# W1's first column pair of each MLP's first quarter as seven half products instead of eight, with the activation combinations formed during the output projection

## The chip, the cores and the metric

The kernel runs as one program on one core of a Trainium2 chip. The metric is the device time of one execution in microseconds (us), lower is better. TensorE (PE) does the matrix products, VectorE (DVE) and ScalarE (ACT) the elementwise work, GpSimd (POOL) a little of it, and the DMA queues of SyncE (SP) and POOL load the weights.

## The reference

A two layer decoder trunk on 256 tokens with 2048 columns in float32. Layer 0 mixes with gated linear attention, layer 1 with sliding window attention on a shared K/V, and each mixer is followed by a square-relu MLP with 8192 hidden columns. What matters here is the border between a mixer's output projection and the MLP behind it, which the program passes twice:

```
h = h + gla_mixer(u, ...)          # ends in  o @ w_o   (layer 1: swa_sink_mixer, o @ w_o)
h = h + sqrelu_mlp(rmsnorm(h, norm_mlp[layer]), mlp_w1[layer], mlp_w2[layer])

def sqrelu_mlp(h, w1, w2):
    u = jax.nn.relu(h @ w1)
    return (u * u) @ w2
```

## The kernel before

**Precision.** Each float32 weight tile is split by `halve` (L107) into a rounded part `wh` (an ACT cast, L116) and a rest `wl` (a DVE subtraction, L117). Activations are kept as such pairs too (`act`: `ah`, `al`). A product is the three matmuls ah wh, ah wl and al wh. In most products the activation is the stationary operand (128 tokens) and 512 columns of the weight move through.

**The MLP.** `mlp` (L952) works in four quarters of 2048 hidden columns. A quarter forms two pairs of 512 columns of W1 and then multiplies with that quarter's rows of W2 (`seven`, L1094). A column pair of W1 is a product of 256 tokens with 2048 x 1024 weights. In `two_columns` (L985, class `Seven`, L219) the upper half of it, a 2 x 2 block product (token halves by two blocks of 512 rows by two blocks of columns), takes seven half products in place of eight. A "product" is 12 matmuls (4 rows of 128, 3 matmuls each), a "plain" step 24, and a pair has seven products and four plain steps, 180 matmuls with 512 moving columns. The steps are named in an order string: "1 21 3 7 5 31 x 20 e 6 2 30 a 4" (a digit is a product, two digits are a plain step on rows block and column block, "x" adds weights for later products). Product 1 uses the weight tile `wx`, which its own queue loads in two halves of 512 KB (`load_x`, L241). Later products use combinations of the weights (accumulating DMAs on POOL, additions on DVE) and of the activations (`es`, tiles `cmb`). The pair's outputs have tokens on the partitions and are turned by 16 transposes (`turn`, L996).

The first pair of the first quarter of each MLP is the exception. There `gemm_wide` (L190) keeps the weight stationary and moves the activations: for each of two columns 64 steps of one matmul with 512 moving columns (ah and al side by side) and one with 256. Its outputs need no transposes, but the row scale of the norm must lie along the free axis, which `along` (L362) does with two matmuls. `pause` (L1058) adds two tiny ones. While it runs, `form_sums` (L972) forms the activation combinations for the other quarters into `cmb` tiles and stores them in DRAM (`kept`), and quarters 1 to 3 fetch them from there with two POOL DMAs each (`fetch_sums`, L979).

**The output projection.** `residual` (L881) multiplies with w_o. Its second column pair is a `Seven` too, in the order "1 21 31 3 7 e 5 20 30 6 2 4"; its last steps are product 6, product 2 and product 4. Product 6 ends the columns of block 3: DVE adds them to the residual (`p56`, L912: `vp`, two `xs`, and as the last one `xs` minus `vp`, L910), then `operands` (L848) turns and scales them into the MLP's `act`. Block 2 follows after product 4. So act 3 is ready before act 2.

**What sets the order.** The code is written step by step with `later` (work put off by so many half steps). A scheduler then places the instructions on each engine, and a wait for a semaphore stands on each instruction that needs one. Each engine and each queue runs its list in order. Tiles come from pools. A mixer’s pool (`g2`/`ga` in layer 0, `s2`/`sa` in layer 1) is closed behind the output projection, and the MLP's pool `mp` (`wx`, `wy`, `u`, `h`) is laid over its memory. The tiles `ws`, `wh`, `wl` and `act` come from pools that live through the whole program.

Of the kernel before, what the change touches and what calls it, by code (L numbers as in the profile page):

```python
# [16 lines left out]
P = 128  # L17
# [22 lines left out]
CS = 13  # L40
RS = 4
MX = 2
COMB = (1, 3)
ORDERS = "1 21 3 7 31 e 5 20 30 6 2 4", "21 1 31 3 7 e 5 20 30 6 2 4"
KEEP = 5, 7
OPS = 7, 9
# [5 lines left out]
def yoco_kernel(ctx: ExitStack, tc: tile.TileContext, x, norms, mlp_w1, mlp_w2, a_w_in, w_glr, w_gate, a_g_o, a_w_o,  # L52
# [12 lines left out]
    def bank(shape, tag, dtype=F32):  # L65
        return ps[tag].tile(shape, dtype, name=tag, tag=tag)
# [94 lines left out]
    def gemm_sta(src, act, evac, widths=(P, P, P, P), first=None):  # L161
# [4 lines left out]
        def run(kq):  # L166
# [16 lines left out]
            if kq == 3:  # L183
                for b, acc in enumerate(accs):
                    evac(b, acc)
        return run

    wide_tags = [("acc",) * 4, ("tp", "ms", "tp", "ms")]

    def gemm_wide(src, act, evac):  # L190

        accs = []
        tags = wide_tags[0]
        wide_tags.reverse()

        def run(kq):
            if kq == 0:
                accs.extend(bank([P, 2, T], tag) for tag in tags)
            halves = split_w(src(kq))
            ah, _, a = act[kq]  # L200
            order = [(k, f) for k in range(4) for f in range(4)]
            if kq == 0:
                order = [(k, 2 * h + f) for h in range(2) for k in range(4) for f in range(2)]
            for i, (k, f) in enumerate(order):
                wh, wl = (w[:, f * P:(f + 1) * P] for w in halves[k])
                mm(accs[f].rearrange("p u t -> p (u t)"), wh, a[:, k].rearrange("p u t -> p (u t)"),
                   kq == 0 and k == 0, False, skip_group_check=True)
                mm(accs[f][:, 1], wl, ah[:, k], False, kq == 3 and k == 3, skip_group_check=True)
                if i == 7:
                    tick()  # L210
            tick()
            if kq == 3:
                for f in range(4):
                    evac(f, accs[f])
        return run
# [146 lines left out]
    def along(rb, r):  # L362
# [6 lines left out]
        nc.scalar.copy(out=rb, in_=pt[:, :T])  # L369

    def twice(rb):
        return rb.rearrange("p (o n) -> p o n", o=1).broadcast_to([P, 2, T])


# [505 lines left out]

    def residual(w, act, gains, first=False, room=None):  # L881


        sq, r = new_norm()
        acts = [{} for _ in gains]
        evacs = [add_to(c, acts, gains, sq, r, 2 if room else 3) for c in range(NC4)]
        runs = [gemm_mov(piece(w, c * C), act, evacs[c]) for c in range(NC4)]
# [9 lines left out]
        es = []  # L897
        if room:
            for b in range(2):
                later(COMB[b], lambda b=b: combine_act(es, act, b, room))  # L900
        for c, kq in ((0, 3), (1, 3)):
            runs[c](kq)
        if not room:
            for c in (2, 3):
                go_all(runs[c])
            return acts, r
        v, wx = room["v"](), room["wx"]()
# [21 lines left out]
    def combine_act(es, act, b, room):  # L929

        bs = slice(2 * b, 2 * b + 2)
        if not es:
            pair = actp.tile([P, 2, 2, 4, P], F32R, name="cmb", tag="act")
            es.extend([pair[:, i] for i in range(2)] + room["es"]())
        us = []
        for c in range(2):
            u = room["u"]()
            nc.vector.tensor_add(out=u, in0=act[c][0].bitcast(F32)[:, bs], in1=act[c][1].bitcast(F32)[:, bs])
            us.append(u)
        combinations(es, bs, us, *(room["e"]() for _ in range(2)))  # L940

# [5 lines left out]
        "u": lambda: g2.tile([P, 2, T], F32, name="xu", tag="oh"),  # L947
        "e": lambda: g2.tile([P, 2, 2, P], F32, name="xe", tag="ol")})
    ga.close()


    def mlp(w1, w2, act, r, gains):  # L952
        mx = ExitStack()
        mp = mx.enter_context(tc.tile_pool(name="mp", bufs=2))
        rb = sm.tile([P, T], F32, name="rb", tag="rb")
        later(RS + 2, lambda: along(rb, r))
        rb2 = twice(rb)
        sq, nr = new_norm() if gains else (None, None)
        acts = [{} for _ in gains]
        wide_tags.sort()  # L960
        vs = [mp.tile([P, C], F32, name=f"v{n}", bufs=1) for n in range(2)]
        dp = mx.enter_context(tc.tile_pool(name="dp", bufs=1, space=bass.MemoryType.DRAM))
        kept = [dp.tile([P, 2, 2, 4, P], F32, name=f"kept{i}") for i in range(2)]
        room = {"u": lambda: mp.tile([P, 2, T], F32, name="m", tag="m"),
                "e": lambda: mp.tile([P, 2, 2, P], F32, name="e", tag="e")}
# [6 lines left out]
        def form_sums(pairs, es, b):  # L972

            combine_act(es, act, b, room)
            if b:
                for a, o in zip(pairs, kept):
                    nc.sync.dma_start(out=o, in_=a.bitcast(F32))

# [68 lines left out]
        def h_rest():  # L1047
# [8 lines left out]
            return at  # L1056

        def pause(n):  # L1058

            pt = small()  # L1060
            for i in range(n):
                mm(pt[:, i:i + 1], ident, ones[:, 0:1])

# [172 lines left out]
        for g in range(4):  # L1236
            w = w2[g * D:(g + 1) * D]
            us, op, uf = {}, None, {}
            op = new_ops()
            sums, es = new_sums()  # L1240
            if g:
                fetch_sums(sums)
                for c in range(2):
                    uf[c] = mp.tile([P, 4, T], F32, name="u", tag="u")

                def put_uf(c, tt, tp, uf=uf):
                    nc.scalar.activation(out=uf[c][:, :, tt], in_=tp, func=AF.Square)

                two_columns([g * D + c * C for c in range(2)], es, h_ops(), put_uf, "1 21 3 7 5 31 x 20 e 6 2 30 a 4")
                for odd in range(2):  # L1250
                    later(OPS[odd], lambda odd=odd, op=op, uf=uf: combine(op, odd, uf))
            else:
                for b in range(2):
                    later(KEEP[b], lambda b=b, sums=sums, es=es: form_sums(sums, es, b))
                later(RS + 3, lambda: pause(2))
                for c in range(2):
                    ms = {}

                    def evac_u(f, acc, c=c, ms=ms, uf=uf, op=op):
                        if f % 2 == 0:  # L1260
                            ms[0] = mp.tile([P, 2, T], F32, name="m", tag="m")
                        if f == 0:
                            uf[c] = mp.tile([P, 4, T], F32, name="u", tag="u")
                        m, j = ms[0], f % 2
                        nc.scalar.copy(out=m[:, j], in_=acc[:, 1])
                        nc.vector.tensor_add(out=m[:, j], in0=acc[:, 0], in1=m[:, j])
                        if j == 0:
                            return
                        bs = slice(f - 1, f + 1)
                        nc.vector.scalar_tensor_tensor(out=m, in0=m, scalar=0.0, in1=rb2, op0=ALU.max, op1=ALU.mult)  # L1270
                        nc.scalar.activation(out=uf[c][:, bs], in_=m, func=AF.Square)
                        if f == 3:
                            combine(op, c, uf)
# [18 lines left out]
    (actk, actq), rstd = mlp(mlp_w1[0], mlp_w2[0], actm, rm, (G_KV, G_MIX1))  # L1292

# [181 lines left out]
    for g in range(4):  # L1475
        go_all(gemm_mov(piece(b_w_q[0], g * C), actq, evac_q2(g)))
        attend(g)

    (actm,), rm = residual(b_w_o[0], acta, (G_MLP1,), False, {
        "v": lambda: s2.tile([P, C], F32, name="vp", tag="hsq"),  # L1480
        "wx": lambda: [s2.tile([P, 2, C], F32, name="wx", tag="sc") for _ in range(2)],
        "es": lambda: [s2.tile([P, 2, 4, P], F32R, name="cmb1", tag="qTt") for _ in range(2)],
        "u": lambda: s2.tile([P, 2, T], F32, name="xu", tag="po"),
        "e": lambda: s2.tile([P, 2, 2, P], F32, name="xe", tag="pv")})
    sa.close()
    mlp(mlp_w1[1], mlp_w2[1], actm, rm, ())


# [41 lines left out]
```

## Time and profile before

| what | value |
| --- | --- |
| median of 3 runs | 2017.98 us (2017.75 to 2019.16) |
| the profiled execution's own time | 2018.76 us |
| its span, first to last instruction | 2016.8 us |
| PE busy | 2001.5 us (99%), 9714 instructions |
| DVE busy | 1752.5 us (87%), 1922 instructions |
| ACT busy | 1308.1 us (65%), 1724 instructions |
| POOL busy | 182.9 us (9%), 199 instructions |
| granted TensorE clock | 1.000 |

The span is 1.96 us shorter than the same execution's time, and that execution lies 0.78 us above the median. A matmul's "busy" time contains its pipeline: matmuls with 512 moving columns show about 0.39 us each but start 0.227 us apart, so PE's cost is read from the starts.

### The profile page before, as it was taken

Reading aid. Unit: us, or ns where it says so; the run is one execution under the profiler, and the core shown is the slowest. Engines: PE = TensorE matmul, PEld = TensorE weight load, DVE = VectorE, ACT = ScalarE, POOL = GpSimd, SP = SyncE. Lnnn points to the kernel's source line nnn. Section 1 sums busy time; section 2 is a strip of 40 time slices with the busy share of each in tenths; the row PEclk is TensorE's granted clock in tenths of the full one; section 3 lists DMA queues with packets and bytes.
Section 4 is the critical chain, followed back from the end, with each engine's and each line's share of the span. In section 5 each row is a group of like instructions: output and inputs, shape, how many; then the busy total and the mean of one; then the engine's idle time right before and its main releaser. Section 6 shows DMA issues by size and latency. Waiting matters only on the chain.

```text
span 2016.8 us, 25788 instructions
## 1 busy us (share of the span) xinstructions
PE 2001.5 (99%) x9714; PEld 1660.9 (82%) x9714; DVE 1752.5 (87%) x1922; ACT 1308.1 (65%) x1724; POOL 182.9 (9%) x199
## 2 busy tenths in 40 slices
PE   9999999999999999999999999999999999999999
PEld 9998888888888888888887878788888888887887
DVE  6698787789989989989999676898889989998998
ACT  6746666667557657656766676666657656755765
POOL 2251110000000000000001121000000000000000
PEclk9999999999999999999999999999999999999999
DMA  8445775796787687778765543687687778778764
GB/s 288 147 157 177 216 222 188 202 291 203 227 273 223 223 264 222 242 241 255 209 202 169 167 135 121 208 285 211 222 261 227 234 245 254 206 230 262 222 225 126
DMA packets 220972, 437.74 MB, mean 217 GB/s; under 512 B 8000, under 2 KB 18512, under 8 KB 218800
## 3 DMA queue, kind: packets, MB, share of 16 engines
q1 hardware_dynamic: 195296, 380.92, 55.4%
q0 software_dynamic: 22464, 53.30, 14.0%
q10 hardware_dynamic: 3088, 1.88, 0.3%
q8 instruction: 76, 1.25, 0.2%
q14 instruction: 48, 0.39, 0.1%
HBM read 429.78 MB, written 6.29 MB: 216 GB/s over the span
## 4 chain that ended last, share of the span: by engine, by line
PE 86%; DVE 7%; ACT 3%; issue 2%; DMA 2%; POOL 0%; SPq 0%; ACTq 0%; POOLq 0%; DVEq 0%
PE acc L83 63%; PE ms L83 14%; PE tp L83 6%; DVE wl L117 3%; PE tp L999 1%; DMA wx<-in_mlp_w_dram 1%; ACT sc L1413 1%; ACT wh L116 1%; DMA ws<-in_a_w_in_dram 1%; DVE wx L1211 0%; PE tp L844 0%; DVE ws L307 0%; DVE sc L1423 0%; PE tp L1345 0%; DVE st L1407 0%
## 5 line engine op out<-in xcount | busy, mean ns | idle before, releaser
L83 PE MATMUL acc<-wh,act 128*128 128x512 f32 x2928 | 938.7, 393 | 0.6 <-DVE xs L1150 0.5
L116 ACT CAST wh<-ws 128x1024 fp32r<-128x1024 f32 x576 | 603.2, 1052 | 339.2 <-PE acc L83 208.2
L117 DVE TENSOR_TENSOR wl<-ws,wh 128x1024 fp32r<-128x1024 f32 x576 | 707.4, 1240 | 100.7 <-ACT wh L116 96.7
L83 PEld LDWEIGHTS acc<-wh,act 128*128 128x128 f32 x2928 | 547.7, 188 | 117.9 <-DVE xs L1150 3.3
L83 PE MATMUL acc<-wl,act 128*128 128x512 f32 x1464 | 570.7, 390 | 1.1 <-DVE wl L117 1.1
L116 ACT CAST wh<-wx 128x1024 fp32r<-128x1024 f32 x272 | 286.0, 1053 | 197.9 <-PE acc L83 140.2
L117 DVE TENSOR_TENSOR wl<-wx,wh 128x1024 fp32r<-128x1024 f32 x272 | 328.0, 1220 | 72.7 <-ACT wh L116 68.5
L83 PEld LDWEIGHTS acc<-wl,act 128*128 128x128 f32 x1464 | 275.1, 188 | 57.0 <-DVE wl L117 1.5
L83 PE MATMUL ms<-wh,act 128*128 128x512 f32 x512 | 166.3, 393 | 0.0
L83 PE MATMUL acc<-act,wh 128*128 128x256 f32 (+1 forms) x640 | 141.4, 308 | 0.5 <-ACT wh L414 0.5
L83 PE MATMUL acc<-wh,ops 128*128 128x512 f32 (+1 forms) x392 | 123.3, 386 | 0.1
L83 PE MATMUL acc<-wh,op 128*128 128x512 f32 x384 | 123.4, 389 | 0.0
L83 PEld LDWEIGHTS ms<-wh,act 128*128 128x128 f32 x512 | 96.1, 188 | 19.5
L83 PEld LDWEIGHTS acc<-act,wh 128*128 128x128 f32 x640 | 104.5, 191 | 6.0 <-ACT wh L414 0.8
L83 PE MATMUL acc<-act,wl 128*128 128x256 f32 x384 | 107.4, 283 | 0.2 <-DVE wl L415 0.2
L83 PE MATMUL ms<-wl,act 128*128 128x512 f32 x256 | 99.7, 390 | 0.0
L83 PE MATMUL tp<-wh,cmb 128*128 128x512 f32 x288 | 94.6, 389 | 0.0
L83 PE MATMUL acc<-wh,cmb 128*128 128x512 f32 x264 | 85.9, 392 | 0.0
L83 PEld LDWEIGHTS acc<-wh,ops 128*128 128x128 f32 x392 | 73.1, 188 | 15.1 <-ACT wh L116 0.6
L83 PEld LDWEIGHTS acc<-wh,op 128*128 128x128 f32 x384 | 72.1, 188 | 15.0
L1112 POOL DMA_DIRECT2D wx<-in_mlp_w_dram x16 | 20.6, 1288 | 656.5 <-DVE wl L117 616.0
L83 PE MATMUL acc<-wl,ops 128*128 128x512 f32 (+1 forms) x196 | 76.3, 389 | 3.1 <-DVE wl L117 3.1
(302 smaller groups left out, 2577.6 us busy)
## 6 DMA issues: line engine op xcount, KB each, us to landing
ws<-in_mlp_w_dram SPq DMA_DIRECT2D x196, 1024.0 KB, 5.4
ws<-in_a_w_in_dram SPq DMA_DIRECT2D x42, 1024.0 KB, 5.1
wy<-in_mlp_w_dram SPq DMA_DIRECT2D x30, 1024.0 KB, 6.6
wx<-in_mlp_w_dram SPq DMA_DIRECT2D x16, 1024.0 KB, 5.2
wx<-in_mlp_w_dram POOLq DMA_DIRECT2D x16, 1024.0 KB, 9.7
ws<-in_b_w_q_dram SPq DMA_DIRECT2D x16, 1024.0 KB, 5.1
ws<-in_a_w_o_dram SPq DMA_DIRECT2D x15, 1024.0 KB, 5.1
ws<-in_b_w_o_dram SPq DMA_DIRECT2D x15, 1024.0 KB, 5.0
```

The source lines that it names most:

```text
L83: nc.tensor.matmul(o, lhsT=l, rhs=r, start=start, stop=stop, **kw)
L116: nc.scalar.copy(out=wh[:, js, :o], in_=w)
L117: nc.vector.tensor_sub(out=wl[:, ks, :o], in0=w, in1=wh.bitcast(F32)[:, js, :o])
L999: nc.tensor.transpose(out=tp[:, k, :], in_=h[:, k * P:(k + 1) * P], identity=ident)
L1112: nc.gpsimd.dma_start(out=ws, in_=block(i, j).rearrange("(k p) n -> p k n", p=P), accum_op=ALU.add)
L1413: nc.scalar.activation(out=sc[:, h], in_=sc[:, h], func=AF.Exp, bias=nmx[:, h:h + 1], scale=f[:, h:h + 1], accum_out=su[:, h:h + 1])
```

## The change

- `gemm_wide`, `along`, `twice`, `pause` and `form_sums` are gone. In every quarter, the first too, the first pair is a `two_columns`. In the first quarter its order is "1 31 21 3 7 5 x 20 e 6 2 30 a 4": the plain step on act 3 comes ahead of the one on act 2.
- The activation combinations that the seven products need are formed in `residual` by a new `keep_act`, 9 and 11 half steps after the first column pair of the output projection. It writes them to `xo` tiles of the mixer's pool (not to `cmb` tiles), and stores them in DRAM with eight DMAs of 256 KB on SP's queue, in place of two of 1 MB.
- The first quarter fetches them with two POOL DMAs as the other quarters do. The tiles `kept` are made ahead of the output projection.

```
-KEEP = 5, 7
+KEEP = 9, 11
...
+        for b in range(2):
+            later(KEEP[b], lambda b=b: keep_act(acts[0], b, room, kept))
         v, wx = room["v"](), room["wx"]()
...
+    def keep_act(act, b, room, kept):
+
+        bs = slice(2 * b, 2 * b + 2)
+        os = room["o"](b)
+        combinations(os, slice(0, 2), sums(act, bs, room), *(room["e"]() for _ in range(2)))
+        for i, o in enumerate(os):
+            nc.sync.dma_start(out=kept[i // 2][:, i % 2, :, bs], in_=o.bitcast(F32))
...
+        "o": lambda b: [g2.tile([P, 2, 2, P], F32R, name="xo", tag="vg"[b], bufs=4) for _ in range(4)]}, kept)
     ga.close()
...
-        later(RS + 2, lambda: along(rb, r))
...
-            if g:
-                fetch_sums(sums)
...
-                go_all(gemm_wide(piece(w1, c * C), act, evac_u))
+            fetch_sums(sums)
+            if g == 0:
+                op = new_ops()
+            for c in range(2):
+                uf[c] = mp.tile([P, 4, T], F32, name="u", tag="u")
+            def put_uf(c, tt, tp, uf=uf):
+                nc.scalar.activation(out=uf[c][:, :, tt], in_=tp, func=AF.Square)
+            two_columns([g * D + c * C for c in range(2)], es, h_ops(), put_uf,
+                        "1 21 3 7 5 31 x 20 e 6 2 30 a 4" if g else "1 31 21 3 7 5 x 20 e 6 2 30 a 4")
```

The order moves at the border between output projection and MLP. On SP's queue, layer 0, before: the last weights of w_o, then four tiles of W1 for the wide products (`ws`), and only then the `wx` of the second pair. (A name in brackets is a semaphore that the row waits for.)

```order
L238 DMA ws_3644<-in_a_w_o_dram 128x4x512 [waits DVE_49]
L128 DMA ws_3736<-in_mlp_w1_dram 128x4x512 [waits DMAHW3_49,DMAHW0_49,DVE_49]
L128 DMA ws_3800<-in_mlp_w1_dram 128x4x512 [waits DMAHW1_49,DVE_49]
L128 DMA ws_3841<-in_mlp_w1_dram 128x4x512 [waits DMAHW2_49,DVE_49]
L128 DMA ws_3908<-in_mlp_w1_dram 128x4x512 [waits DMAHW3_49,DVE_49]
L248 DMA wx_4192<-in_mlp_w1_dram 128x2x512 [waits DMASW4_49,DMASW3_49,DMASW5_49,DMASW2_49,DMASW6_49,DMASW1_49,DMASW7_49,DMASW0_49,DMAHW7_49,DVE_49,PE_49]
L248 DMA wx_4192<-in_mlp_w1_dram 128x2x512
```

The same place in the changed kernel. The `wx` here is the first pair's, for product 1:

```order
L208 DMA ws_3829<-in_mlp_w1_dram 128x4x512 [waits DMAHW0_49,DVE_49]
L208 DMA ws_3873<-in_mlp_w1_dram 128x4x512 [waits DMAHW1_49,DVE_49]
L912 DMA kept01_2919<-xo_3578 128x2x256 [waits DMAHW7_49,DVE_49]
L912 DMA kept01_2919<-xo_3579 128x2x256 [waits DVE_49]
L208 DMA ws_3927<-in_mlp_w1_dram 128x4x512 [waits DMAHW2_49,DVE_49]
L912 DMA kept00_2918<-xo_3635 128x2x256 [waits DVE_49]
L912 DMA kept00_2918<-xo_3636 128x2x256 [waits DMAHW3_49,DVE_49]
L912 DMA kept01_2919<-xo_3637 128x2x256 [waits DMAHW4_49,DVE_49]
L912 DMA kept01_2919<-xo_3638 128x2x256 [waits DMAHW5_49,DVE_49]
L218 DMA wx_3789<-in_mlp_w1_dram 128x2x512 [waits DMASW7_49,DMASW6_49,DMAHW0_49,DMASW5_49,DMAHW2_49,DMASW4_49,DMAHW3_49,DMASW3_49,DMAHW4_49,DMASW2_49,DMAHW5_49,DMASW1_49,DMAHW6_49,DMASW0_49,DMAHW7_49,DVE_49,PE_49]
L218 DMA wx_3789<-in_mlp_w1_dram 128x2x512
```

`wx` now stands behind the stores of `kept`, and its wait names the DMA semaphores that those stores raise (DMAHW2 to DMAHW5) beside DVE and PE. In both kernels the value of DVE that the first `wx` waits for is that of the subtraction of `vp` from `xs` (L910 before, L873 now).

On PE, layer 0, before, from the last matmuls of product 4 (`act_2256`) into the wide products (`acc_3732`, `acc_3733`), with the transposes of act 3 (`tp`) among them:

```order
L83 MATMUL acc_3505<-wl_3679,act_2256 128x512
L83 MATMUL acc_3505<-wh_3678,act_2256 128x512
L83 MATMUL acc_3732<-act_3335,wh_3738 128x512 [waits Activation_49]
L83 MATMUL acc_3732<-act_3335,wl_3740 128x256 [waits DVE_49]
L83 MATMUL acc_3733<-act_3335,wh_3738 128x512
L83 MATMUL acc_3733<-act_3335,wl_3740 128x256
L83 MATMUL acc_3732<-act_3335,wh_3738 128x512
L844 MATMUL tp_3667<-ident_79,xs_3309 128x128 [waits DVE_49,PE_49]
```

And now, from the same product 4 through all 16 transposes of act 3 and act 2 into product 1 (`acc_3792`) and the plain step on act 3 (`acc_3838`, `acc_3839`):

```order
L82 MATMUL acc_3509<-wl_3735,act_2256 128x512
L82 MATMUL acc_3509<-wh_3734,act_2256 128x512
L810 MATMUL tp_3723<-ident_79,xs_3313 128x128 [waits DVE_49,PE_49]
L810 MATMUL tp_3723<-ident_79,xs_3313 128x128 x3
L810 MATMUL tp_3752<-ident_79,xs_3313 128x128 x4
L810 MATMUL tp_3812<-ident_79,xs_3271 128x128 [waits DVE_49,PE_49]
L810 MATMUL tp_3812<-ident_79,xs_3271 128x128 x3
L810 MATMUL tp_3852<-ident_79,xs_3271 128x128 [waits DVE_49,PE_49]
L810 MATMUL tp_3852<-ident_79,xs_3271 128x128 x3
L82 MATMUL acc_3792<-wh_3793,act_3339 128x512 [waits Activation_49]
L82 MATMUL acc_3792<-wl_3795,act_3339 128x512 [waits DVE_49]
```

Between product 4 and the MLP's first matmul there are now only the transposes, and that first matmul needs the ACT cast of `wx`. On ACT the casts of `wx` (`wh_3793`, `wh_3794`) stand ahead of the cast of the plain step's weights, which SP's queue has asked for long before:

```order
L322 ACTIVATE act_3817<-tp_3812,gT_88 128x256 [waits PE_49]
L115 CAST wh_3793<-wx_3789 128x1024 [waits DMAHW5_49,DMAHW4_49,DMAHW6_49,DMAHW3_49,DMAHW7_49,DMAHW2_49,DMAHW0_49]
L322 ACTIVATE act_3817<-tp_3812,gT_88 128x256 [waits DVE_49]
L115 CAST wh_3794<-wx_3789 128x1024 [waits DMAHW7_49]
L115 CAST wh_3831<-ws_3829 128x1024
```

The border of layer 1 is moved in the same way.

More of the change, by code (lines that the diff above doesn't have):

```diff
@@ L40 @@
 CS = 13
-RS = 4
 MX = 2
@@ L185, in run @@
                     evac(b, acc)
[L186 to L214, printed above, removed]
         return run
@@ L879, in rstd_of, with residual @@
         rsqrt(r, v[:, 1], v[:, 0], 1.0 / D, NT)
-    def residual(w, act, gains, first=False, room=None):
+    def residual(w, act, gains, first, room, kept):
         sq, r = new_norm()
         acts = [{} for _ in gains]
-        evacs = [add_to(c, acts, gains, sq, r, 2 if room else 3) for c in range(NC4)]
+        evacs = [add_to(c, acts, gains, sq, r, 2) for c in range(NC4)]
         runs = [gemm_mov(piece(w, c * C), act, evacs[c]) for c in range(NC4)]
@@ L897, in residual @@
         es = []
-        if room:
-            for b in range(2):
-                later(COMB[b], lambda b=b: combine_act(es, act, b, room))
+        for b in range(2):
+            later(COMB[b], lambda b=b: combine_act(es, act, b, room))
         for c, kq in ((0, 3), (1, 3)):
             runs[c](kq)
[L903 to L906, printed above, removed]
+        for b in range(2):
+            later(KEEP[b], lambda b=b: keep_act(acts[0], b, room, kept))
         v, wx = room["v"](), room["wx"]()
@@ L934, in combine_act, with sums, new_kept @@
             es.extend([pair[:, i] for i in range(2)] + room["es"]())
-        us = []
-        for c in range(2):
-            u = room["u"]()
+        combinations(es, bs, sums(act, bs, room), *(room["e"]() for _ in range(2)))
+    def sums(act, bs, room):
+        us = [room["u"]() for _ in range(2)]
+        for c, u in enumerate(us):
             nc.vector.tensor_add(out=u, in0=act[c][0].bitcast(F32)[:, bs], in1=act[c][1].bitcast(F32)[:, bs])
-            us.append(u)
-        combinations(es, bs, us, *(room["e"]() for _ in range(2)))
+        return us
+    def keep_act(act, b, room, kept):
[4 more added lines that the diff above has]
+            nc.sync.dma_start(out=kept[i // 2][:, i % 2, :, bs], in_=o.bitcast(F32))
+    dp = ctx.enter_context(tc.tile_pool(name="dp", bufs=1, space=bass.MemoryType.DRAM))
+    def new_kept(n):
+        return [dp.tile([P, 2, 2, 4, P], F32, name=f"kept{n}{i}") for i in range(2)]
+    kept = new_kept(0)
     (actm,), rm = residual(a_w_o[0], acto, (G_MLP0,), True, {
@@ L1056, in h_rest @@
             return at
[L1058 to L1062, printed above, removed]
         def new_ops():
@@ L1237, in mlp @@
             w = w2[g * D:(g + 1) * D]
-            us, op, uf = {}, None, {}
-            op = new_ops()
+            us, uf = {}, {}
+            if g:
+                op = new_ops()
             sums, es = new_sums()
-            if g:
-                fetch_sums(sums)
[L1243 to L1273, printed above, removed]
-                    go_all(gemm_wide(piece(w1, c * C), act, evac_u))
@@ new lines, in mlp @@
+            fetch_sums(sums)
+            if g == 0:
+                op = new_ops()
+            for c in range(2):
[4 more added lines that the diff above has]
+                        "1 21 3 7 5 31 x 20 e 6 2 30 a 4" if g else "1 31 21 3 7 5 x 20 e 6 2 30 a 4")
+            for odd in range(2):
+                later(OPS[odd], lambda odd=odd, op=op, uf=uf: combine(op, odd, uf))
@@ L1477, in yoco_kernel @@
         attend(g)
+    kept = new_kept(1)
     (actm,), rm = residual(b_w_o[0], acta, (G_MLP1,), False, {
```

26 lines of the change are left out of this document (7 added, 19 removed).

## The prediction

> **What bounds the kernel now.** I read the page's totals and its chain first, then the two borders between output projection and MLP.
>
> ```profile
> span 2016.8 us, 25788 instructions
> PE 2001.5 (99%) x9714; PEld 1660.9 (82%) x9714; DVE 1752.5 (87%) x1922; ACT 1308.1 (65%) x1724; POOL 182.9 (9%) x199
> PEclk9999999999999999999999999999999999999999
> PE 86%; DVE 7%; ACT 3%; issue 2%; DMA 2%; POOL 0%; SPq 0%; ACTq 0%; POOLq 0%; DVEq 0%
> ```
>
> TensorE is busy in 99% of the span at full clock and holds 86% of the chain that ended last. So a matmul removed saves its place on PE, and anything that makes PE wait is paid in full. The next view gives the busy time in three stretches: the wide pair of layer 0 (from its first matmul to the first of the next pair), that of layer 1, and, from quarter 1 of layer 0, a first pair made with seven products.
>
> ```profile
> core 0: us, PE busy (x) PEld busy (x) DVE busy (x) ACT busy (x) POOL busy (x), PEclk, DMA share, GB/s
> 405.25:452.83 47.58, 47.55 (x282) 41.54 (x280) 41.48 (x66) 29.10 (x52) 3.25 (x3) 1.00 0.93 299
> 1330.21:1377.80 47.59, 47.57 (x282) 41.83 (x281) 41.68 (x66) 29.30 (x53) 3.23 (x3) 1.00 0.92 299
> 578.16:620.17 42.01, 42.01 (x189) 34.36 (x188) 37.09 (x35) 27.04 (x32) 3.55 (x3) 1.00 0.85 260
> ```
>
> PE has no gap in any of them. The wide pair takes 47.58 us, the pair with seven products 42.01 us. The two can't be subtracted yet, since they hold different side work. PE's rows in order of time (start, duration) show it:
>
> ```profile
> 405.25 0.39 PE L83 MATMUL acc<-act,wh 128*128 128x512 f32 x1
> ...
> 412.55 0.60 PE L844 MATMUL tp<-ident,xs 128*128 128x128 f32 x4
> 412.90 0.48 PE L83 MATMUL acc<-act,wh 128*128 128x512 f32 x1
> 413.22 0.28 PE L83 MATMUL acc<-act,wl 128*128 128x256 f32 x1
> ...
> 452.83 0.39 PE L83 MATMUL acc<-wh,act 128*128 128x512 f32 x1
> ...
> 620.17 0.60 PE L999 MATMUL tp<-ident,h 128*128 128x128 f32 x4
> 620.53 0.48 PE L83 MATMUL acc<-wh,act 128*128 128x512 f32 x1
> 620.84 0.40 PE L83 MATMUL acc<-wl,act 128*128 128x512 f32 x1
> ```
>
> Four transposes and the matmul behind them take 0.67 us, from 412.55 to 413.22 and from 620.17 to 620.84. A matmul with 512 moving columns starts 0.227 us after the one before (42.01 us hold 180 of them and two groups of four transposes), so a group costs 0.44 us. The wide pair contains 16 transposes of `operands`, four groups, about 2.0 us with what PE drains ahead of them. The seven pair contains two of its own four `turn` groups. The other two fall behind its end.
>
> **The change part by part.**
>
> *Removed.* The wide pair with all that lies in it: 47.58 us in each MLP.
>
> *Added on PE.* The pair with seven products, 42.0 us, and its two later turns, 2 x 0.44 = 0.9: together 42.9 us. The 16 transposes of `operands` now stand ahead of product 1 (order on PE), 2.0 us. If nothing waited, the border would take 2.0 + 42.9 = 44.9 in place of 47.6: 2.7 us less in each MLP, 5.4 in all. That is the most that the change can win.
>
> *A new wait: product 1 needs `wx`.* Before, the wide products needed `ws` tiles, asked for long ahead. `wx` lies in the memory of the mixer's pool. When it may start shows on the rows of the first `wx` load of each MLP, then needed only some 40 us later, and of the DVE subtraction (L910) in front of it. The last row is from the queue's list of waits (us in total, times, longest):
>
> ```profile
> 406.14 0.68 DVE L910 TENSOR_TENSOR xs<-xs,vp 128x512 f32<-128x512 f32 x1
> 406.89 0.88 SPq L248 DMA_DIRECT2D wx<-in_mlp_w_dram  x2
> 1331.09 0.69 DVE L910 TENSOR_TENSOR xs<-xs,vp 128x512 f32<-128x512 f32 x1
> 1331.91 0.88 SPq L248 DMA_DIRECT2D wx<-in_mlp_w_dram  x2
> SPq L248 <- DVE xs L910: 1.2, 2, 0.6
> ```
>
> The subtraction ends at 406.82, the load is issued at 406.89. Product 4, the last of the output projection, gives way to the MLP at 405.25. So even at the old place `wx` starts 1.64 us after PE has run out of the projection. How long it then takes to land (one DMA, min/median/max alike):
>
> ```profile
> L248 SPq DMA_DIRECT2D wx<-in_mlp_w_dram x1: 368/368/368, 406.9 to 406.9; - x1
> DMA to landing us min/median/max: 5.3/5.3/5.3
> ...
> L248 SPq DMA_DIRECT2D wx<-in_mlp_w_dram x1: 368/368/368, 576.6 to 576.6; - x1
> DMA to landing us min/median/max: 6.0/6.0/6.0
> ...
> L116 ACT CAST wh<-wx 128x1024 fp32r<-128x1024 f32 x272 | 286.0, 1053 | 197.9 <-PE acc L83 140.2 <-issue 11.8 <-PE ms L83 10.8
> L117 DVE TENSOR_TENSOR wl<-wx,wh 128x1024 fp32r<-128x1024 f32 x272 | 328.0, 1220 | 72.7 <-ACT wh L116 68.5
> ```
>
> 5.3 us for the very transfer in question, then a cast of 1.05. The plain step on act 3 can't fill the hole: its weights are in, but on PE it stands behind product 1, and on ACT its cast stands behind those of `wx`.
>
> *The start of `wx` moves later.* Two things now lie ahead of it. First DVE: the second half of `keep_act` must be formed in the last steps of the projection. DVE's rows there before, and the sizes of such additions and subtractions:
>
> ```profile
> 395.76 1.23 DVE L331 TENSOR_TENSOR wx<-wx,ws 128x1024 f32<-128x1024 f32 x1
> 396.90 1.22 DVE L117 TENSOR_TENSOR wl<-ws,wh 128x1024 fp32r<-128x1024 f32 x1
> ...
> 411.78 1.28 DVE L938 TENSOR_TENSOR m<-act 128x512 f32<-128x512 f32 x2
> ...
> 421.19 1.09 DVE L722 TENSOR_TENSOR cmb<-e,cmb 128x256 fp32r<-128x256 f32 x3
> ```
>
> After 396.90 the changed order has on DVE four `wl` (1.14 apart), one sum of activations (0.60), eight short ones (0.34 each), then `vp`, three `xs` and the subtraction (0.60 each): 4.6 + 0.6 + 2.7 + 3.0 = 10.9, so the subtraction ends near 407.9, about 1.1 later than before. The last `wl` of product 4 then comes up to 0.4 us after PE wants it, which is inside this reckoning, since I count from the old 405.25. Second, the stores of `kept`, which the wait names too. The last one follows the eighth short operation, near 404.9, and SP needs some 0.4 us for each issue:
>
> ```profile
> kept<-cmb SPq DMA_DIRECT2D x4, 1024.0 KB, 6.5
> out_dram<-xt SPq DMA_DIRECT2D x3, 256.0 KB, 2.4
> ws<-in_kv_w_k_dram SPq DMA_DIRECT2D x4, 512.0 KB, 3.8
> ```
>
> A store of 256 KB lands 2.4 us after its issue by the nearest row, a larger one 6.5. I take 2.4 because the size is equal; with an issue near 405.4 that is 407.8. So `wx` starts near 408.2. The bounds: it can't start before product 2 has ended (2.72 us ahead of 405.25) and four DVE operations after it (2.5), which is 405.1; and it starts at 409.0 if the stores take a microsecond more.
>
> *The wait in numbers.* 408.2 + 5.3 + 1.05 + 0.1 for the hand-over = 414.65: product 1 begins 9.4 us after 405.25, in which the 16 transposes are hidden. Its second matmul needs `wl` of the same half, 1.24 us after the cast, of which one matmul covers 0.23: 1.0 less what is left of handing over, I take 0.9. Behind that ACT and DVE deliver halves every 1.05 and 1.14 us, and PE takes at least 1.36 for six matmuls, so nothing more is lost there.
>
> *Moved at no cost.* `along`, `pause` and the combinations leave the wide pair with it (they are in the 47.58). The two fetches of 1 MB on POOL's queue start once the stores have landed. Their first user, product 3 or 7, comes after product 1 and most of two plain steps, some 50 x 0.227 = 11 us after product 1's start, near 426. `wx`, the two fetches, `wy` and the next `wx` are 5 MB, and the queues moved these bytes in forty slices after 404 us:
>
> ```profile
> GB/s 160 12 0 0 0 152 168 234 351 335 406 390 375 378 421 394 410 273 312 285 324 382 402 398 414 406 402 343 180 191 277 324 347 417 339 218 191 293 355 386
> ```
>
> At 400 GB/s 5 MB take 13 us from 408, so they land by 421. If this cover went, each microsecond late would be one on PE. DVE gains three weight halvings and the weight additions in this pair, but in quarter 1 the same pair has DVE busy for 37.1 of 42.0 us, and the hole ahead of product 1 gives it time for `operands`.
>
> *Sum for one MLP.* 9.4 + 0.9 + 42.0 + 0.9 = 53.2, against 47.6: 5.6 us more. Layer 1 has the same rows (1330.21, 1331.91), so twice that, 11.2 us. The profiled execution took 2018.76 (span 2016.8), 0.78 above the median of 2017.98, and would take 2030.0. Against the median that is 2029.2, and I forecast 2029.
>
> **A rule about shared DMA engines.** The first half of `wx` landed in 5.3 us with a `ws` load of 1 MB ahead of it on its own queue, and in 6.0 in the other row. The Trainium skill, "DMA: Bandwidth & Descriptors", section "Queues, rings and completion order", says that each DMA engine takes turns between the queues that have work, a packet at a time. By that rule the fetch on POOL's queue, which starts at the same moment, takes every second turn from `wx`, and the sum would be 2031.8 in place of 2029.2. No run here shows the two together yet. It is the second rival below, which is priced from the rows alone.
>
> **The rivals.**
>
> *`wx` starts as early as its inputs allow* (the combinations fit in DVE's gaps, the stores land early). Then 405.1 + 5.3 + 1.15 = 411.6, 6.3 us after 405.25, and with the second matmul's wait hidden 6.3 + 42.9 = 49.2: 1.6 more in each MLP, 2021.2. Against it: the eight short operations have to go somewhere, and before the change DVE's rows from 396.90 to 406.82 stood nearly end to end.
>
> *The fetch shares the engines with `wx`.* 512 KB at about 400 GB/s are 1.3 us, so an equal share adds 1.3 to the landing: 2 x 1.3 more, 2031.8. For it speaks the common release by the stores, against it that POOL's issue takes longer and so comes behind.
>
> *The first quarter is slowed further*, by late combinations or by DVE. Three microseconds in each MLP give 2035. It decides where the fetches land after 426.
>
> *The other side: PE hardly waits.* If product 1 could start within 2.66 us of product 4's end, or another product filled the hole, the change would win more than 4 us, up to 5.4, and come to 2012.6. Against it: the chain of DVE, SP's queue, landing and cast is in every row above and sums to at least 6.3 at the landing seen here. Even the fastest 512 KB row of the page (`kv_w_k`, 3.8) would leave 4.8.
>
> That the change saves no matmuls can't be: the pair's 180 are fixed in the code.
>
> **How the numbers follow.** Forecast (2029, between 2024 and 2033): 0.57. Shared engines (2031.8): 0.20. Slowed further (2035): 0.08. Early start (2021.2): 0.10. Hardly a wait (2012.6): 0.05. A measurement of this kernel can tell about 0.2%, 4.0 us, from no change. So slower has 0.57 + 0.20 + 0.08 = 0.85, no change 0.10 and faster 0.05. The range goes from 2021, which takes in the early start, to 2035; the faster case stays out.
>
> **What would show it.** Right: PE idle for 6 to 9 us at both borders, ended by the cast of `wx`, and `wx` issued 2 to 4 us after the projection's last matmul. ACT waits for the DMA of `wx` there. The pair itself, from product 1 to its end, takes about 42 us, and the quarters after it are as before. Wrong: product 1 starting within 5 us of product 4, or PE's idle time at another place, such as product 3 or 7 waiting for `cmb`. If the wait is there and the time is still as before, the saving on PE was larger than 2.7 us in each MLP.

## The result, and the profile after

The changed kernel takes 2048.7 us (median of 4 runs, 2047.75 to 2049.58) against 2017.87 for the kernel before on the same chip (2017.0 to 2019.16). The ratio is 1.0152, with a 95% interval of 1.0135 to 1.0170: 30.7 us slower, 15.3 in each MLP. The forecast was 2029, 5.6 more in each MLP. The sign was right, the size was not: the range ended at 2035.

The profiled execution took 2049.58. From the page, in the order of the prediction's first fence:

```profile
span 2047.9 us, 25613 instructions
PE 2006.2 (98%) x9578; PEld 1654.2 (81%) x9578; DVE 1774.6 (87%) x1928; ACT 1321.1 (65%) x1732; POOL 190.4 (9%) x207
PEclk9999999989999999999999999989999999999999
PE 78%; DVE 8%; issue 7%; DMA 4%; ACT 3%; POOL 0%; ACTq 0%; SPq 0%; POOLq 0%; DVEq 0%
```

PE's share of the chain has fallen from 86% to 78%. There are 136 matmuls fewer, and still PE is "busy" 4.7 us longer. The row of the granted clock gives one reason: it has an 8 in two of forty slices, and these hold the two borders. PE's rows at the border of layer 0 that waited for something (start, duration, and in brackets the idle time and what ended it):

```profile
400.98 0.50 PE L82 MATMUL acc<-wl,act 128*128 128x512 f32 x1 [0.81 <-DVE wl L116]
405.53 0.50 PE L82 MATMUL acc<-wl,act 128*128 128x512 f32 x1 [1.17 <-DVE wl L116]
410.16 1.07 PE L810 MATMUL tp<-ident,xs 128*128 128x128 f32 x8 [1.74 <-DVE xs L826]
413.38 1.06 PE L810 MATMUL tp<-ident,xs 128*128 128x128 f32 x8 [2.15 <-DVE act L323]
421.16 0.79 PE L82 MATMUL acc<-wh,act 128*128 128x512 f32 x1 [6.72 <-ACT wh L115]
422.42 0.79 PE L82 MATMUL acc<-wl,act 128*128 128x512 f32 x1 [0.47 <-DVE wl L116]
```

Up to 399.78, the start of product 2, the two traces run together (399.81 before). Products 2 and 4 now end late, since `wl` comes late. Then come the 16 transposes, and at 421.16 product 1, 15.9 us after the old 405.25. Its first matmuls show 0.79 us where 0.39 is usual. The chain of work that ended last, at the same border (start, us, what):

```profile
406.95 0.68 DVE xo L688 x2
...
407.76 3.62 DMA kept<-xo
...
411.59 8.30 DMA wx<-in_mlp_w_dram
...
420.06 1.05 ACT wh L115
...
421.14 1.24 DVE wl L116
```

`wx` waits for the last store of `kept` to land, and takes 8.30 us itself. In layer 1 the store is in time, and DVE's last subtraction releases `wx`, which then takes 8.91:

```profile
1352.25 0.61 DVE xs L873
...
1352.99 8.91 DMA wx<-in_mlp_w_dram
```

Busy time by stretches around product 1 of layer 0 (the number behind POOL's is the granted clock, then the share of the DMA engines):

```profile
408.00:414.00 6.00, 2.11 (x16) 1.51 (x15) 5.28 (x12) 4.20 (x12) 1.13 (x2) 1.00 0.77 251
414.00:428.00 14.00, 6.82 (x19) 4.91 (x17) 6.76 (x8) 6.25 (x8) 3.76 (x3) 0.51 1.04 365
428.00:432.00 4.00, 4.00 (x19) 3.26 (x19) 2.63 (x2) 2.60 (x3) 0.00 (x0) 1.00 1.10 241
```

For 14 us TensorE had half its clock, and half of these it was working. Product 1, the two plain steps and products 3 and 7 are 84 matmuls, 19.1 us at 0.227; from 421.16 they take 23.1. So in layer 0 the border costs 15.9 until product 1 starts, 42.9 for the pair with its turns, and 4.0 for the clock and a late `wl`, against 47.6: +15.2. The turns of the second pair lie 15.4 us behind those of before. In layer 1, counted from product 2 of its projection, which starts 18.7 us later than before, the same sum is 14.2 + 42.9 + 3.9 - 47.4 = +13.6, and the turns lie 13.3 further behind. The rest, some 2 us, is a net: some 3.3 us are lost between the two borders, and about 1 is regained behind the second.

### The profile page after: what moved, and what is told of

It reads as the page before. It is cut to its first block, busy times and chain, and to the rows that moved or that the text cites. A ratio compares the mean times of both kernels' runs of the same rounds, so it can differ in the third digit from the quotient of the medians.

```text
span 2047.9 us, 25613 instructions
## 1 busy us (share of the span) xinstructions
PE 2006.2 (98%) x9578; PEld 1654.2 (81%) x9578; DVE 1774.6 (87%) x1928; ACT 1321.1 (65%) x1732; POOL 190.4 (9%) x207
## 4 chain that ended last, share of the span: by engine, by line
PE 78%; DVE 8%; issue 7%; DMA 4%; ACT 3%; POOL 0%; ACTq 0%; SPq 0%; POOLq 0%; DVEq 0%
PE acc L82 58%; PE ms L82 12%; PE tp L82 5%; DVE wl L116 4%; DMA wx<-in_mlp_w_dram 3%; PE tp L963 1%; ACT wh L115 1%; ACT sc L1350 1%; DMA wx<-in_a_w_o_dram 1%; DVE ws L277 1%; DVE xs L1107 0%; DMA ws<-in_a_w_in_dram 0%; DVE sc L1360 0%; PE tp L1282 0%; DMA xt<-in_x_dram 0%
## 5 line engine op out<-in xcount | busy, mean ns | idle before, releaser
L82 PE MATMUL acc<-wh,act 128*128 128x512 f32 x3104 | 1000.4, 395 | 14.4 <-ACT wh L115 13.0
L82 PEld LDWEIGHTS acc<-wh,act 128*128 128x128 f32 x3104 | 583.5, 189 | 140.5 <-ACT wh L115 14.0
L82 PE MATMUL acc<-wl,act 128*128 128x512 f32 x1552 | 608.0, 392 | 5.4 <-DVE wl L116 5.3
L115 ACT CAST wh<-wx 128x1024 fp32r<-128x1024 f32 x288 | 302.5, 1053 | 213.8 <-PE acc L82 144.7
L116 DVE TENSOR_TENSOR wl<-wx,wh 128x1024 fp32r<-128x1024 f32 x288 | 347.6, 1222 | 84.1 <-ACT wh L115 80.5
L82 PEld LDWEIGHTS acc<-wl,act 128*128 128x128 f32 x1552 | 293.0, 189 | 67.9 <-DVE wl L116 8.8
L82 PE MATMUL tp<-wh,cmb 128*128 128x512 f32 x320 | 105.1, 389 | 0.0
L82 PE MATMUL acc<-act,wh 128*128 128x256 f32 x512 | 95.3, 285 | 1.3 <-ACT wh L380 1.3
L82 PEld LDWEIGHTS acc<-act,wh 128*128 128x128 f32 x512 | 80.6, 191 | 1.6 <-ACT wh L380 1.5
L116 DVE TENSOR_TENSOR wl<-wy,wh 128x1024 fp32r<-128x1024 f32 x64 | 76.1, 1221 | 1.1 <-ACT wh L115 1.1
```

Of the source, the lines that this page charges most:

```text
L82: nc.tensor.matmul(o, lhsT=l, rhs=r, start=start, stop=stop, **kw)
L115: nc.scalar.copy(out=wh[:, js, :o], in_=w)
L116: nc.vector.tensor_sub(out=wl[:, ks, :o], in0=w, in1=wh.bitcast(F32)[:, js, :o])
```

## The experiments

The excess is (ratio - 1) x 2018 us; the ratio is to the kernel before on the same chip, so the medians of two rows can't be compared directly.

| kernel | median us | ratio, 95% interval | excess |
| --- | --- | --- | --- |
| changed kernel | 2048.70 | 1.0152 (1.0135 to 1.0170) | 30.7 |
| plain steps first | 2041.55 | 1.0106 (1.0091 to 1.0122) | 21.4 |
| sums formed early | 2039.78 | 1.0098 (1.0085 to 1.0112) | 19.8 |
| filler, 30 matmuls | 2047.68 | 1.0137 (1.0123 to 1.0151) | 27.6 |
| filler, 44 matmuls | 2047.63 | 1.0134 (1.0119 to 1.0150) | 27.0 |
| product 1's weights apart | 2036.96 | 1.0086 (1.0071 to 1.0100) | 17.4 |
| projection half alone | 2026.47 | 1.0036 (1.0023 to 1.0049) | 7.3 |
| MLP half alone | 2037.24 | 1.0091 (1.0077 to 1.0105) | 18.4 |
| MLP half, weights apart | 2032.81 | 1.0071 (1.0057 to 1.0085) | 14.3 |
| sums early, weights apart | 2033.07 | 1.0072 (1.0060 to 1.0085) | 14.5 |
| no fetch in the first quarter | 2039.60 | 1.0099 (1.0085 to 1.0112) | 20.0 |
| sums early, weights apart, fetch behind | 2033.25 | 1.0065 (1.0053 to 1.0078) | 13.1 |
| the same, sums on GpSimd | 2042.49 | 1.0113 (1.0100 to 1.0127) | 22.8 |

**The projection half alone.** The wide pair stays, the combinations are formed and stored in the projection.

```
 KEEP = 9, 11          # keep_act in residual, as changed
+            sums, es = new_sums()
+            fetch_sums(sums)          # all four quarters
 ...
                     go_all(gemm_wide(piece(w1, c * C), act, evac_u))
```

> Only the half of the change that is in the projection: the first quarter's pair stays one of eight half products (32 matmuls of each weight block), the combinations are formed and stored in the output projection and read back in all four quarters. Theory A (in products 2 and 4 VectorE is short of time, and 3.0 us are lost there whatever follows; the wide pair's weights wait in buffers of their own, so that nothing waits for wx): 3 to 4 us in each MLP, 6 to 9 over the kernel before (2024 to 2027). Theory B (the whole loss of the changed kernel comes from the border's order, and VectorE's delay would be hidden by the wide pair): within 2 of the kernel before. Theory C (the reading of 2 MB beside the weights delays the wide pair too): 10 or more over it.

Measured: an excess of 7.3, as theory A had it. At the end of the first pair of layer 0 it was 4.0. PE waits at the same two places as in the changed kernel, and nothing at this border waits for `wx`:

```profile
401.06 0.50 PE L83 MATMUL acc<-wl,act 128*128 128x512 f32 x1 [0.68 <-DVE wl L117]
405.61 0.50 PE L83 MATMUL acc<-wl,act 128*128 128x512 f32 x1 [1.15 <-DVE wl L117]
```

Products 2 and 4 take 8.35 us here in place of 5.44. So some 3 of these 4 us are VectorE's lateness there: `keep_act` stands between the `wl` that PE wants.

**The MLP half alone.** The combinations are formed in the first steps of the MLP; there are no stores in the projection and no fetch in the first quarter.

```
-KEEP = 9, 11
+KEEP = 1, 2
...
+            if g:
+                fetch_sums(sums)
+            else:
+                for b in range(2):
+                    later(KEEP[b], lambda b=b, sums=sums, es=es: form_sums(sums, es, b))
```

> Only the half that is in the MLP: seven half products in the first quarter's first pair, with the combinations formed in the MLP's first steps (half steps 1 and 2) as part of that quarter, stored there, and read in quarters 1 to 3 alone. Theory A (the late issue of wx comes from the sums and stores in the projection, its slow landing from the combinations' reading, and products 2 and 4 stretch for the sums alone): products 2 and 4 are as before, wx is issued at about 407 and lands in 5 to 6 us, product 1 starts 8 to 9 us after the old place, and with 2 to 4 us of half clock and sums the time is 8 to 12 us above the kernel before in each MLP less the 4.7 that the shorter pair brings: 8 to 14 over it in all (2026 to 2032). Theory B (the pair's start is set by the turned activations): as the changed kernel, 25 to 31 over the kernel before.

Measured: 18.4, between the two theories. The part on `wx` went better than theory A said: it is issued at 405.93 (about 407 was expected) and lands in 4.0 us (5 to 6 were expected). Its issue (SP) and its cast (ACT):

```profile
405.93 0.88 SPq L218 DMA_DIRECT2D wx<-in_mlp_w_dram  x2
409.94 1.04 ACT L115 CAST wh<-wx 128x1024 fp32r<-128x1024 f32 x1 [0.21 <-DMA wx<-in_mlp_w_dram]
```

What theory A missed are waits inside the pair: in product 3 PE waits 1.02 us for a cast and 0.94 for a `wl`. The halves' sum, 7.3 + 18.4 = 25.7, is 5 short of the 30.7 of both together. That fits with the late stores ahead of `wx` and the fetch beside it, which stand in PE's way only where both halves do; no run takes this sum apart.

**No fetch in the first quarter.** This isolates what the fetch does to `wx`.

```
-            sums, es = new_sums()
-            fetch_sums(sums)
+            if g:
+                sums, es = new_sums()
+                fetch_sums(sums)
+            else:
+                es = [act[c][2].rearrange("p k u n -> p u k n")[:, :, :, t * P:(t + 1) * P]
+                      for c in range(2) for t in range(NT)]
```

> The changed kernel without the reading of the combinations in the first quarter: its products 3, 7, 5 and 6 take activations in their place, of the same shape (the output is then another one); the sums and their stores stay. Theory A (the 2 MB read on GpSimd's queue share the transfer engines with wx, which then lands 8.5 us after its issue; without them it lands 4.0 us after it, as in the kernel with the MLP's half alone): product 1 starts 4 to 5 us earlier, and the time is 8 to 11 us below the changed kernel, 20 to 23 over the kernel before. Theory B (the price of 1.3 us in each MLP at which the forecast's rival put this): 2 to 4 us below the changed kernel. Theory C (wx lands late because its issue is late, whatever else is read): no difference over 2.

Measured: 20.0, which is 10.7 below the changed kernel: theory A. The store is as late as in the changed kernel and `wx` is issued at the same moment, but it lands in 3.97 us in place of 8.30 (the chain again):

```profile
407.97 3.57 DMA kept<-xo
...
411.74 3.97 DMA wx<-in_mlp_w_dram
```

PE waits 1.46 us for the cast in place of 6.72, and product 1 starts 4.2 us earlier.

**The sums formed early.**

```
-KEEP = 9, 11
+KEEP = 5, 7
```

> The combinations are formed two products earlier in the output projection (half steps 5 and 7 in place of 9 and 11). Theory A (VectorE is late with the low halves of products 2 and 4, which costs 3.0 us before the border, and as late with the stores, so that wx is issued 3.4 us later than forecast): both go, 6 to 8 us in each MLP, and the time is 2033 to 2037. Theory B (VectorE is full over the whole projection, and the sums stand in the way of products 6 and 20 as much): the time stays at 2045 to 2050.

Measured: 19.8, 10.9 below the changed kernel. That is nearer to theory A, but 2.8 us outside its range. The waits for `wl` in products 2 and 4 are gone, as it said. But in layer 1 PE now waits 1.44 us for a cast and 1.55 for `xs` around product 6, so theory B has a part in it. In layer 0 `wx` is issued at 408.13, about the moment that the prediction had for the changed kernel, and still product 1 starts at 416.30:

```profile
408.13 0.89 SPq L218 DMA_DIRECT2D wx<-in_mlp_w_dram  x2
415.20 1.05 ACT L115 CAST wh<-wx 128x1024 fp32r<-128x1024 f32 x1 [4.06 <-DMA wx<-in_mlp_w_dram]
416.30 0.79 PE L82 MATMUL acc<-wh,act 128*128 128x512 f32 x1 [4.41 <-ACT wh L115]
```

The landing takes 7.0 us here: the fetch went out at 402.5 and 403.8 and its second half landed at 413.4, five microseconds after the issue of `wx`.

**Two fillers for the clock.** Matmuls whose result nobody reads, ahead of product 1; the second kernel has 44 of them.

```
+        def fill(a, n=30):
+            pt = small()
+            for i in range(n):
+                mm(pt, identr, a[:, 0].rearrange("p u t -> p (u t)"))
...
+                fill(act[3][2])
```

> 30 matmuls of 512 columns whose result nobody reads (about 6.8 us) stand behind the first eight turns and ahead of product 1; everything that product 1 waits for stays. Theory A (the clock granted after the idle time, 0.50 and 0.70 for some 9 us where the records show 0.79 us for a matmul of 0.39, is caused by the idle time itself): with TensorE kept busy the clock stays at 1.00, and about 3 to 4 us of each MLP come back: 2040 to 2043. Theory B (the low clock costs nothing, because product 1 waits for its halves from VectorE anyway, or does not hang on idle time): 2047 to 2052, the filler's own time where it ends after wx.

> 44 matmuls of 512 columns in place of the first filler's 30 (10.0 us in place of 6.8), so that TensorE is busy until wx has been cast and nothing is waited for behind the filler. Theory A (the halved clock comes from idle time in the microseconds before, so the first filler, which left 2.5 us idle ahead of product 1, only moved it): the granted clock is 1.00 through the whole border, product 1 runs at 0.23 us a matmul, starts up to 2 us later than in the changed kernel and gains the 3.8 us of the low clock: 2 to 3 us less in each MLP than the changed kernel, 24 to 27 over the kernel before. Theory B (the clock hangs on something else, or the matmuls behind wait for VectorE's low halves at any clock): no gain, and the 2 us on top, 31 to 36 over the kernel before.

Measured: 27.6 with 30. The median of 2047.68 lies in theory B's range, but it settles nothing: the filler ended before `wx` was cast, PE idled 2.51 us more, and the clock then fell within product 1. With 44 it is 27.0, theory A's upper edge; the interval overlaps that of the changed kernel, so the trace of one execution has to decide. Granted clock ahead of the filler, at its start, and from there on:

```profile
405.00:411.00 6.00, 3.44 (x16) 2.50 (x17) 5.90 (x10) 1.82 (x5) 0.21 (x1) 1.00 0.97 322
411.00:415.00 4.00, 3.35 (x12) 2.54 (x11) 2.74 (x7) 2.96 (x10) 0.91 (x2) 0.62 0.73 235
416.00:430.00 14.00, 14.00 (x65) 11.38 (x64) 8.21 (x7) 6.97 (x8) 3.76 (x3) 1.00 1.05 337
```

The waits at the transposes still pull the clock down, and the filler itself brings it up again. Product 1 starts at 423.94, 2.8 us later than in the changed kernel, runs at 0.231 us a matmul, and the second pair's turns come 0.7 us earlier all the same. So the half clock is a consequence of the idle time. In layer 0 it costs 3 to 3.5 us on top of it: 3.0 by the changed kernel's own rows (4.0 less the wait for `wl`), 2.8 + 0.7 = 3.5 by this comparison. The filler's own length takes back the most of it.

**Product 1's weights apart.**

```
+            if self.apart:
+                p = self.product("A", self.token(0, 0), self.load(0, 0))
+                self.load_x(0, 0, False)
```

> Product 1 takes its weights from a buffer of the seven-product streams, read early by a load of its own, and wx itself is read behind it for the products that follow (1 MB more to read in each MLP); product 1 stands directly behind product 4. Theory A (the wait is for wx, whose place in the mixer's memory comes free late and whose landing shares the engines with the combinations' reading): product 1's 12 matmuls run at the old place, the turns behind it wait under it, and the 6.7 us and most of the low clock go: 8 to 10 us in each MLP, 2029 to 2033. Theory B (the turns themselves, waiting on VectorE and ScalarE, are what is late): 3 to 5 us in each MLP, 2039 to 2043.

Measured: 17.4, 13.3 below the changed kernel, between the theories. Product 1 follows product 4 at once. What is left are the 0.37 and 1.16 for `wl` in products 2 and 4, 1.37 at the transposes, and then waits of up to 1.94 at product 3, whose `wy` lands late.

**The plain steps first.**

```
-"1 31 21 3 7 5 x 20 e 6 2 30 a 4"
+"31 21 1 3 7 5 x 20 e 6 2 30 a 4"
```

> The first quarter begins with its two plain steps (24 matmuls of 512 columns each, about 10.9 us together at the 0.227 us of the profile), whose weights wait in buffers of their own, and product 1, which reads wx, comes behind them. Theory A (in the changed kernel wx is read too late, and the 6.7 us in which product 1's halves are awaited, with the halved clock behind them, are paid on the path): nearly all of both goes, 8 to 10 us in each MLP, and the time is 2029 to 2033. Theory B (the turned activations of the last two column blocks are as late as wx, so that the plain steps wait in its place): under 2 us in each MLP, 2045 to 2049.

Measured: 21.4, 9.3 below the changed kernel, so neither theory. Nothing waits for `wx` any more, but 4.54 us are waited for `xs` ahead of the transposes and up to 1.28 for the turned activations.

**Cures together.** The MLP half with the weights apart, and the early sums with the weights apart:

> The half in the MLP (combinations formed there) with product 1's weights in a buffer of their own and product 1 directly behind product 4, ahead of the turns. Theory A (what was left at the border with wx apart was VectorE's lateness in products 2 and 4, 3 us, and the reading of the combinations, which delays wy and the weights of the products that use them, about 4 us): both go, and the first pair lies between the old one and 3 us later in each MLP: 0 to 6 over the kernel before (2018 to 2024). Theory B (VectorE cannot form the combinations and the low halves of seven products in the same 20 us): 8 to 14 over it, as with the MLP's half alone.

> Product 1's weights in a buffer of their own as before, and the combinations formed two products earlier in the projection. Theory A (the two cures are for different waits and add up: 14.6 us less with wx apart, 11.7 less with the earlier sums, of which the part for wx, about 6, is the same): 9 to 13 over the kernel before (2027 to 2031). Theory B (with wx apart nothing else waits for the stores, and the border is bound by what is read there, 2 MB of combinations beside the weights at a share of 1.05 of the transfer engines): no more than 2 us under the kernel with wx apart alone, 14 to 17 over the kernel before.

Measured: 14.3 and 14.5, theory B both times (the first at its upper edge). In the first one VectorE has no free time left from 400 to 440 us (the sum of a table by stretches), and PE waits where an activation is late:

```profile
sum 40.00, PE 36.37 PEld 28.89 DVE 39.79 ACT 27.64 POOL 3.20; mean PE 4.55 PEld 3.61 DVE 4.97 ACT 3.46 POOL 0.40
421.60 1.43 PE L82 MATMUL acc<-wh,act 128*128 128x512 f32 x3 [2.63 <-DVE act L327]
```

In the second one a load of `ws` goes out together with the fetch and lands in 8.9 us (5.9 in the changed kernel, where no fetch goes with it). ACT stands 3.75 us before its cast, and the scaling of the activations stands behind that cast: PE waits 3.37 us for it.

**The fetch behind the weights, and the sums on GpSimd.**

```
+            then = None if g else lambda sums=sums: fetch_sums(sums, nc.sync)    # called behind wy's load
...
+        combinations(os, slice(0, 2), sums(act, bs, room, nc.gpsimd), *(room["e"]() for _ in range(2)), nc.gpsimd)
```

> The kernel with the sums formed early and product 1's weights apart, in which the first quarter's combinations are now read on SyncE's queue behind wx and wy. Theory A (weights that are awaited first then land first, and the combinations still come in time for product 3, 13.6 us behind product 1's start): 2 to 4 us less in each MLP than with the reading on GpSimd's queue, 6 to 10 over the kernel before. Theory B (the border has a fixed number of bytes to read and VectorE's work as its second bound, so that the wait moves to products 3 and 7): within 2 of that kernel, 12 to 16 over the kernel before.

> As the one before it, and the sums and differences of the activations (2 additions and 4 subtractions for each half, some 3 us of VectorE's 4.5 for a half) are formed on GpSimd, which is 9% busy. Theory A (VectorE's time around the border is what still holds the pair up): 2 to 4 us less in each MLP than the one before it. Theory B (with the sums at half steps 5 and 7 VectorE has caught up by product 4, so that taking them away there changes nothing at the border, or GpSimd is so slow that the stores and the reading come later): no gain, or some us more.

Measured: 13.1 and 22.8, in the times theory B twice. The first moves the wait to product 3:

```profile
427.16 0.47 PE L82 MATMUL acc<-wh,cmb 128*128 128x512 f32 x1 [2.19 <-DMA cmb<-kept]
```

At the border of layer 0 this kernel has lost 3.7 us (the turns of the second pair), at that of layer 1 another 9.0. PE's longest waits there are 2.24 us for the fetch and 1.28 and 1.56 around product 6 of the projection, for a cast and for `xs`. In the second kernel a subtraction of 128x256 takes 0.76 or 1.26 us on GpSimd by its medians, on VectorE 0.42. PE waits up to 2.49 us for a `wl` in layer 0's projection and 3.06 in layer 1's. In layer 0 the first transposes already come 8.0 us later than in the kernel without GpSimd's sums (418.49 against 410.50), so the loss lies ahead of the border.

No version came below the kernel before. The best that has the shorter pair is 13.1 over it.

## Why the prediction was right in sign and wrong in size

- **Right: the mechanism.** Product 1 waits for the cast of `wx`, ACT waits for the DMA of `wx`, and PE's idle time ahead of it (6.72 and 6.31 us) lies in the 6 to 9 us that were named as the sign. The pair is 42.0 plus what the prediction and the next points add. The 2.7 us less on PE in each MLP fit the sum above, but no run shows them alone. The later quarters cost 2 us net, which the prediction put at nothing; the largest of these waits in the first MLP is 0.88 for `xs` at 579.41, and its cause was not tried. A slip without weight: the second pair of layer 1 begins at 1377.58, so the wide pair there is 47.4 and not 47.6.
- **Wrong: "`wx` starts near 408.2".** It started at 411.59 in layer 0. Two terms failed. DVE was to finish the eighth short operation near 404.9, which was 407.6. The stretch itself was reckoned rightly: four `wl`, one sum and eight short operations took 7.9 us. But it began at 399.71 in place of 396.90. An addition of weights (1.1 us) that lay ahead of it before had moved into its way. And the cast that DVE waited for came 1.8 us later (the first row below is the kernel before, the others the changed one; the DVE row is the first of the four `wl`):

```profile
393.42 1.05 ACT L116 CAST wh<-wx 128x1024 fp32r<-128x1024 f32 x1 [3.08 <-DMA wx<-in_a_w_o_dram]
395.21 1.05 ACT L115 CAST wh<-wx 128x1024 fp32r<-128x1024 f32 x1 [2.97 <-DMA wx<-in_a_w_o_dram]
399.71 1.22 DVE L116 TENSOR_TENSOR wl<-ws,wh 128x1024 fp32r<-128x1024 f32 x1
```

  The read of w_o's `wx` that this cast waits for was issued when it was before (383.9), but landed after 11.2 us in place of 9.4. In all eleven kernels that store `kept` in the projection it took 10.6 to 12.4 us, in the three that don't (before, and the two with the MLP half) 8.6 to 9.5; no run tries these stores alone. The prediction looked at what the second half's sums and stores do, and not at the stores of the first. The other term: a store of 256 KB was to land in 2.4 us by the row of the output's stores; it took 3.62. By DVE alone `wx` would have started near 410.6.
- **Wrong: the last `wl` of product 4 "up to 0.4 us after PE wants it".** Products 2 and 4 lost 3.0 us in layer 0, 0.81 and 1.17 of it in one piece, and 1.6 in layer 1. In the changed kernel this is hidden behind the wait for `wx`; the projection half alone pays it.
- **Wrong: "5.3 us for the very transfer in question".** It took 8.30 and 8.91. The prediction had the reason as a rival, with a chance of 0.20 and 1.3 us in each MLP. Taking the fetch out brought the landing to 3.97 and the time down by 10.7, 5.3 in each MLP. The rival's price was 512 KB of the fetch at the full rate. But while the first 512 KB of `wx` were landing, GpSimd's queue moved 2.05 MB, nearly the whole fetch, and SyncE's 0.83 MB. The Trainium skill, "DMA: Bandwidth & Descriptors", section "Queues, rings and completion order", has the engines take turns between queues by the packet. The runs agree that the two are mixed, 3.97 us without the fetch's queue and 8.30 with it, but by bytes the shares were 5 to 2. The trace counts 272 packets of 7.5 KB for the fetch's queue there and 423 of 2.0 KB for SyncE's, so a turn of the fetch carried more; that this made the shares is an inference, and no run tests it.
- **Wrong: "nothing more is lost there"** behind product 1. The 0.9 forecast for the second matmul's `wl` was right (it started 1.26 us after the first, 1.03 more than the usual 0.23), but together with the halved clock 4.0 and 3.9 were lost. The prediction took the row of a clock at 1.00 for granted while it forecast 6 to 9 us without work. The Trainium skill, "TensorE: Matmul & The Clock Gate", Part 1, says that the clock is halved after an idle window of about 3.4 us and comes back after about as long of work. The trace agrees on the way back: the second filler had the clock back 3.2 us after its start. On the fall it differs: the clock fell near 414.4, behind waits of 1.74 and 2.15 us with eight transposes between them and eight behind, each wait shorter than that window, and in the kernel with the MLP half and the weights apart one wait of 2.63 us was enough.

Together, in layer 0: 9.4 became 15.9 (3.4 by the late start of `wx`, 3.0 by its landing), 0.9 became 4.0, and 5.6 became 15.2. In layer 1 the start has 1.1 of it and the landing 3.6.

## What to carry to other kernels

Where an operand's load is put on the path, its landing time must be read from a moment with the same company on the DMA engines, and a new load beside it is part of its price. A forecast idle time of TensorE of some microseconds is to be priced with the halved clock that follows. Before a step is moved to an engine's "free" time, its neighbours' due times there matter more than the engine's busy share: VectorE was 87% busy, and wherever the 7.8 us of combinations (2 x (2 x 0.60 + 8 x 0.34)) were tried, in the projection's last or middle steps or in the MLP's first, PE waited for something behind them.

## What the runs showed of the hardware

- The granted clock fell to 0.50 within 6 us of scattered waits (1.74 and 2.15 us, from 408.4 on, with eight transposes between), stayed there for nearly 14 us, and a matmul of 0.39 us then showed 0.79. A single wait of 2.63 us was followed by the half clock too.
- 512 KB landed in 4.0 us with 512 KB and `wy` behind it on its own queue, in 7.0 to 8.9 with a read of 2 MB on GpSimd's queue as well, at a DMA share of 1.04. In the 8.3 us of one such landing GpSimd's queue moved 2.05 MB and SyncE's 0.83.
- An accumulating read of 512 KB on GpSimd's queue landed in 8.6 to 9.5 us (three kernels), and in 10.6 to 12.4 with stores of 256 KB on SyncE's queue beside it (eleven kernels).
- The 44 filler matmuls, 11.95 us in the trace, cost no time that the runs can tell (27.0 over the kernel before, against 30.7 without them): product 1 started 2.8 us later, and more than that came back through the clock.
